# Four plain column tiles and five block pairs in the out-projection of a hybrid decoder layer

## The chip, the cores and the metric

The kernel runs on one core of a Trainium2 chip. The metric is the device time of one execution in microseconds (us): the median of three runs before the change is 2372.61 us (2370.54 to 2372.68).

## The reference, cut to what matters

A decoder layer over 16 learned tokens and 512 inputs, with 2048 features. Two head groups work side by side, a short convolution and a recurrent one; their 2048 output columns are multiplied by `w_out`, normalised and added to the input. A gated feed-forward layer follows. The change lies in the product with `w_out`.

```python
z = n @ w_in
y_conv = short_conv_group(z[..., :CONV_COLS], conv_w)
y_rwkv = rwkv7_group(z[..., CONV_COLS:], ...)
mix = jnp.concatenate([y_conv, y_rwkv], axis=-1) @ w_out      # 528 x 2048 by 2048 x 2048
h = h + rmsnorm(mix, g_post_mix)
f = conv_glu(rmsnorm(h, g_pre_ffn), w_gate_up, conv_ffn, w_down)
h = h + rmsnorm(f, g_post_ffn)
```

## The kernel before, in words

Everything is held transposed: 128 features on the partitions, tokens along the free axis. For the out-projection 514 tokens count, in two halves of 258 and 256 columns (`HY`). Products are made to float32 accuracy from two rounded parts of each operand, a high and a low one, as three matmuls: high by high, high by low, low by high.

The out-projection has 16 column tiles of 128 features each, `m` = 0 to 15, in three groups (lines 1384 to 1491):

- **Plain tiles**, `m` = 0 to `MS`-1 with `MS` = 6 (line 1386). `gemm` (line 552) goes over 16 feature tiles `k`, three part products and two token halves: 96 matmuls of 128x258 or 128x256. A tile's weights come as four chunks of 128x512 (`w_out`, 256 KB each); `wload` (line 543) loads a chunk into `raw` (three buffers, shared with other users), ScalarE casts the high part `whi` and VectorE subtracts to get the low part `wlo` (three buffers each).
- **Pairs**, four of them: `m` = 6 to 13, two tiles at a time (`pair`, line 1426). The weights of two tiles and the tokens are seen as 2 by 2 blocks, and the four products of blocks that two tiles need are made of seven products instead of eight. One product (`product`, line 1415) is 8 feature tiles by three part products, 24 matmuls of 258 columns, so a pair has 168. Its four weight blocks of 128x1024 (`w_pair`, 512 KB each) are loaded in the order a22, a21, a11, a12 into the tag `R`, which has five buffers; VectorE makes the sums and differences of blocks (`plus`, `less`), and `parted` (line 1352) makes a block's high part `H` and low part `O` (three buffers each). The first product of a pair uses a11 with tokens that are in place; the second a12; the third uses the token sums `T2`, the fifth `T3`, the sixth `T4`, and the last the block sum `s1` with `Y1`.
- **The last two tiles**, `m` = 14 and 15, by token halves.

The token sums that the pairs need are made once, by `sums(j)` for `j` = 0 to 7 (line 1371): two loads of 257 KB from `ysp` (the head groups' output in DRAM) into `R` (into `H` and `O` for `j` = 0), three VectorE sums or differences of 258 columns into `q`, `O` or `R`, and three splits, each a ScalarE cast and a VectorE subtraction into a `tt` block. Which plain tile a sum is made with stands in `JS` (line 85): `JS[m]` sums are written ahead of tile `m`. `Y1` is made after the plain tiles in a loop of eight (`again`, lines 1401 to 1408): a load into a `raw` buffer, a difference and a split that overwrites the tokens' second half, so it has to wait for the last plain tile to have read that half.

What sets the order: from line 1387 on, for `m` >= `MP` = 2, instructions are not issued as written but kept in a plan (`Plan`), and ordered by a list scheduler with modelled costs (`order`, `run`); the plan's start sets TensorE busy for the first `HEAD` = 8.0 us. The plan reaches from tile 2 over all pairs, the residual and the first feed-forward work, to line 1858. What is written before it, tiles 0 and 1 with what stands ahead of them, is placed by the framework's own scheduler, among the end of the plan before (the recurrent heads). The `matmul` steps carry the rank `FILL`: TensorE takes them when nothing of a higher rank is ready, so a plain tile's matmuls can lie between the products of a pair.

`layout` (lines 1992 to 1995) cuts `w_out` on the host by `MS`: columns of the plain and the last tiles as `w_out`, the rest as `w_pair`.

All engine calls go through one helper, so the profile shows every instruction at line 231; instructions are told apart by their tiles.

Of the kernel before, what the change touches and what calls it, by code (L numbers as in the profile page):

```python
# [78 lines left out]

K0, K1 = 4, 2  # L80

MS = 6


MP, JS, HEAD = 2, (0, 0, 3, 3, 2, 0), 8.0

GSUMS = (0, 4, 8, 12)

# [422 lines left out]
def hymba(tc, I, out, ysp=None):  # L511
# [40 lines left out]
    def gemm(src, mov, spans, first=None, into=None, kept=None, parts=1):  # L552


        for ku in range(KT // 4):
            if kept is not None:
                hi, lo = kept[ku]
            else:
                hi, lo = wload(src[ku], into and into[ku]) if ku or first is None else first
            for k4 in range(4):  # L560
                k = ku * 4 + k4
                ws = slice(k4 * 128, k4 * 128 + 128)
                xh, xl = mov[k]
                for pi, (w, x) in enumerate(((hi, xh), (hi, xl), (lo, xh))):
                    for o, a, b in spans:
                        PE.matmul(o, w[:, ws], x[:, a:b], start=(k == 0 and pi == 0),
                                  stop=(k == KT - 1 and pi == 2))
                    if pi == 2 or parts == 3:
                        yield

    def run(g):
        for _ in g:
            pass

    def fill(g):

        g = iter(g)
        while True:
            with plan.step(2, FILL):
                try:  # L580
                    next(g)
                except StopIteration:
                    return
            yield
# [669 lines left out]
    with ExitStack() as ctx2:  # L1254
# [43 lines left out]
        def mixed(x, m, i):  # L1298
            a, b = HY[i]
            sq[i] = ss[i] if m == 0 else small(b - a)  # L1300
            with plan.step(0 if m >= KT - 2 else 2):
                S.activation(out=sq[i], in_=x, func=AF.Square)
            if 0 < m < KT - 1:
                G.tensor_tensor(out=ss[i], in0=ss[i], in1=sq[i], op=ALU.add)
            S.activation(out=h[:, m, a:b], in_=x, func=AF.Copy, scale=pc("g_post", m))
# [26 lines left out]
        def half(ps, i):  # L1332
            a, b = HY[i]
            return [(ps[i][:, :b - a], a, b)]
# [50 lines left out]
        plan.head = HEAD  # L1385
        for m in range(MS):
            plan.on = m >= MP
# [38 lines left out]
        def pair(n):  # L1426


            a22, a21, a11, a12 = (load(I["w_pair"][n, i]) for i in (3, 2, 0, 1))
            s1 = big("R", F32)  # L1430
            plus(s1, a21, a22)
            k = two()

            def row(r, i, o, k=None):
                m = MS + 2 * n + r
                a, b = HY[i]
                o = o[:, 2 * i:]
                if k is not None:
                    plus(h[:, m, a:b], o, k[:, 2 * i:])
                    o = h[:, m, a:b]  # L1440
                mixed(o, m, i)

            c = product(a11, Y11, mp.tile([128, 2, 512], F32, name="mps")[:, 0, :258])
            S.copy(k[:, 0], c)
            row(0, 0, product(a12, Y21), k[:, 0])
            less(a11, s1, a11)
            product(a11, Y2, c, False)
            S.copy(k[:, 1], c)
            less(a21, a22, a11)
            less(a11, a12, a11)  # L1450
            plus(k[:, 1], product(a11, Y22), k[:, 1])
            product(a21, Y3, c, False)
            S.copy(k[:, 0], c)
            product(a22, Y4, c, False)
            row(1, 0, c)
            o = product(s1, Y1)
            row(0, 1, o, k[:, 1])
            row(1, 1, o, k[:, 0])

        for n in range((KT - 2 - MS) // 2):  # L1460
            pair(n)
# [4 lines left out]
        for n, m in enumerate(range(KT - 2, KT)):  # L1466
# [4 lines left out]
            else:  # L1471
                t = mp.tile([128, 2, 512], F32, name="mps")
                ps = [t[:, i] for i in range(2)]
            run(fill(gemm(I["w_out"][m - KT + 2 + MS], ys, half(ps, 0), into=keep)))
            mixed(half(ps, 0)[0][0], m, 0)
# [493 lines left out]
def layout(np, inp):  # L1969
# [6 lines left out]
    def tiles(w):  # L1976
        k, n = w.shape
        return w.reshape(k // 512, 4, 128, n // 128, 128).transpose(3, 0, 2, 1, 4).reshape(n // 128, k // 512, 128, 512)
# [13 lines left out]
    w = A["w_out"].reshape(KT, 128, D)[list(KORD)].reshape(D, D)  # L1992
    a, b = 128 * MS, D - 256
    r["w_out"] = tiles(np.concatenate([w[:, :a], w[:, b:]], axis=1))
# [51 lines left out]
```

## Time and profile before

| | before |
|---|---|
| median of three runs | 2372.61 us |
| the profiled execution's own time | 2370.47 us |
| its span, first to last instruction | 2368.7 us |
| first plain load of `w_out` / first load of `w_pair` | at 773.27 / 833.05 us |
| tile 2's first matmul | at 808.65 us |
| first pair's first matmul | at 848.30 us |

The span and the time of the same execution differ by 1.8 us. A row of a timeline has the start, the duration, the engine, the operation with `out<-in`, the shape, the count of merged instructions and, in brackets, the idle time of the engine before it with what ended it. Matmuls overlap: their pitch is read from the starts. A row of the stretches has, after the length, the busy time and count of TensorE (PE), its weight loads (PEld), VectorE (DVE), ScalarE (ACT) and GpSimd (POOL), then the granted TensorE clock, the share of the DMA engines and GB/s. SP is the queue that issues most DMAs; an SP row with several loads spans from the first issue to the last.

### The profile page before, as it was taken

The page shows a single profiled execution, that of the slowest core. Times are in us where ns is not written, and L with a number is a line of the kernel's source. Part 1 is how long each engine was busy: PE and PEld are TensorE (multiplying, and loading weights), DVE is VectorE, ACT ScalarE, POOL GpSimd, SP SyncE. Part 2 cuts the span into 40 slices and gives each one's busy share as a digit, 9 for nine tenths or more (in the row PEclk, how much of TensorE's full clock was granted, in tenths as well). Part 3 has the DMA queues.
Part 4 walks back from the last instruction along what each step waited for, and adds up shares of the span by engine and source line. Part 5 has one row for each costly group of instructions (what it writes and reads, how often), then busy time and mean ns, then how long its engine had stood idle before and what let it go on. Part 6 is the DMA issues. An engine that isn't in the chain of part 4 may idle for free.

```text
span 2368.7 us, 46298 instructions
## 1 busy us (share of the span) xinstructions
PE 2345.2 (99%) x18450; PEld 2238.2 (94%) x18450; DVE 1744.6 (74%) x2366; ACT 1225.2 (52%) x2402; POOL 636.1 (27%) x755
## 2 busy tenths in 40 slices
PE   9999999999999999999999999999999999999997
PEld 8999999999999999998989899999999998989897
DVE  7687888878754677784868686777767686859585
ACT  7666766766654555574434343343434342525255
POOL 0232747465351011510202121211212120202025
PEclk9999999999999999999999999999999999999998
DMA  5444332333433755913333323242423242323344
GB/s 185 158 126 122 90 97 83 104 111 98 132 99 95 232 170 178 214 57 100 108 107 103 112 82 124 81 134 81 124 75 125 70 135 79 124 82 105 97 142 90
DMA packets 138759, 274.14 MB, mean 116 GB/s; under 512 B 31120, under 2 KB 54288, under 8 KB 138544
## 3 DMA queue, kind: packets, MB, share of 16 engines
q1 hardware_dynamic: 131760, 264.35, 36.2%
q0 software_dynamic: 6784, 6.83, 2.0%
q8 instruction: 145, 2.38, 0.4%
q14 instruction: 70, 0.57, 0.1%
HBM read 245.30 MB, written 25.84 MB: 114 GB/s over the span
## 4 chain that ended last, share of the span: by engine, by line
PE 96%; DVE 1%; DMA 1%; POOL 1%; ACT 1%; issue 0%; DVEq 0%; SPq 0%; ACTq 0%; POOLq 0%
PE mps L231 60%; PE u L231 18%; PE d L231 11%; PE st L231 4%; PE aux L231 3%; DMA acc<-xT_dram 1%; DVE acc L231 0%; POOL acc L231 0%; PE psn L231 0%; DVE q L231 0%; DMA l<-lo 0%; DMA raw<-w_in_dram 0%; ACT whi L231 0%; POOL XR L231 0%; ACT q L231 0%
## 5 line engine op out<-in xcount | busy, mean ns | idle before, releaser
L231 ACT CAST H<-R 128x1024 fp32r<-128x1024 f32 x401 | 420.4, 1049 | 474.9 <-PE u L231 180.7
L231 DVE TENSOR_TENSOR O<-R,H 128x1024 fp32r<-128x1024 f32 x401 | 521.7, 1301 | 124.2 <-ACT H L231 116.8
L231 PE MATMUL mps<-ahi,whi 128*128 128x264 f32 (+2 forms) x1792 | 360.0, 289 | 6.1 <-ACT ahi L231 5.5
L231 PE MATMUL mps<-alo,whi 128*128 128x264 f32 (+2 forms) x1792 | 360.2, 289 | 0.0
L231 PE MATMUL mps<-ahi,wlo 128*128 128x264 f32 (+2 forms) x1792 | 358.0, 288 | 1.2 <-DVE wlo L231 1.0
L231 PE MATMUL mps<-tt,H 128*128 128x258 f32 x2160 | 288.2, 283 | 1.0 <-ACT q L231 0.9
L231 PEld LDWEIGHTS mps<-ahi,whi 128*128 128x128 f32 x1792 | 273.8, 189 | 9.1 <-ACT ahi L231 5.8
L231 PEld LDWEIGHTS mps<-ahi,wlo 128*128 128x128 f32 x1792 | 274.0, 189 | 3.6 <-DVE wlo L231 1.6
L231 PEld LDWEIGHTS mps<-alo,whi 128*128 128x128 f32 x1792 | 274.0, 189 | 2.8 <-DVE alo L231 0.6
L231 DVE TENSOR_TENSOR wlo<-raw,whi 128x512 fp32r<-128x512 f32 x261 | 199.2, 768 | 104.8 <-ACT whi L231 88.0
L231 PEld LDWEIGHTS mps<-tt,H 128*128 128x128 f32 x2160 | 272.6, 189 | 2.4 <-ACT q L231 1.1
L231 POOL TENSOR_TENSOR raw<-raw,rb 128x516 f32<-128x516 f32 (+1 forms) x45 | 92.8, 2062 | 668.7 <-DVE raw L231 630.6
L231 PE MATMUL mps<-alo,H 128*128 128x258 f32 x1064 | 258.3, 284 | 0.4 <-DVE alo L231 0.4
L231 PE MATMUL mps<-ahi,H 128*128 128x258 f32 x1064 | 258.0, 282 | 0.0
L231 POOL TENSOR_TENSOR R<-R 128x1024 f32<-128x1024 f32 x40 | 131.5, 3287 | 419.1 <-DVE R L231 419.1
L231 ACT CAST whi<-raw 128x512 fp32r<-128x512 f32 x261 | 160.7, 619 | 137.5 <-PE mps L231 83.9
L231 DVE TENSOR_TENSOR R<-R 128x1024 f32<-128x1024 f32 x136 | 226.4, 1665 | 1.7 <-DMA R<-w_pair_dram 0.4
L231 PEld LDWEIGHTS mps<-alo,H 128*128 128x128 f32 x1064 | 198.4, 189 | 0.9 <-DVE alo L231 0.6
L231 PEld LDWEIGHTS mps<-ahi,H 128*128 128x128 f32 x1064 | 198.7, 190 | 0.0
L231 POOL TENSOR_SCALAR SUV<-VT 32x64 f32<-32x64 f32 x272 | 129.4, 476 | 161.4 <-PE st L231 137.5
L231 PE MATMUL mps<-ahi,O 128*128 128x258 f32 x1064 | 157.5, 283 | 0.0
L231 PE MATMUL mps<-tt,O 128*128 128x258 f32 x1080 | 153.4, 281 | 0.0
(339 smaller groups left out, 4593.5 us busy)
## 6 DMA issues: line engine op xcount, KB each, us to landing
R<-w_gu_dram SPq DMA_DIRECT2D x176, 512.0 KB, 3.5
raw<-w_in_dram SPq DMA_DIRECT2D x208, 256.0 KB, 2.7
R<-w_down_dram SPq DMA_DIRECT2D x88, 512.0 KB, 3.7
raw<-w_out_dram SPq DMA_DIRECT2D x32, 256.0 KB, 3.6
R<-w_pair_dram SPq DMA_DIRECT2D x16, 512.0 KB, 4.3
l<-lo SPq DMA_DIRECT2D x24, 264.0 KB, 2.1
R<-ysp SPq DMA_DIRECT2D x14, 257.0 KB, 4.3
lo<-l SPq DMA_DIRECT2D x12, 264.0 KB, 2.6
```

The source lines that it names most:

```text
L231: return getattr(self.real, op)(*real, **{k: x.get() if isinstance(x, View) else x for k, x in kw.items()})
```

## The change

Two lines of constants:

```diff
-MS = 6
+MS = 4
-MP, JS, HEAD = 2, (0, 0, 3, 3, 2, 0), 8.0
+MP, JS, HEAD = 2, (0, 2, 3, 3), 8.0
```

Tiles 4 and 5 are no longer plain: the pairs now cover `m` = 4 to 13, five of them (`range((KT - 2 - MS) // 2)`, line 1460). The eight sums are written ahead of tiles 1, 2 and 3 (two, three, three) instead of 2, 3 and 4 (three, three, two). Since `MP` stays 2, the first two sums now stand outside the plan. The host layout follows `MS`: 24 chunks of `w_out` and 20 blocks of `w_pair` instead of 32 and 16. All else is as it was, though the plan from tile 2 on is made anew.

## The prediction

> **What bounds the kernel now.** I read the page first, for the bound, then the stretches around the out-projection, then the waits of TensorE there, then the timelines of TensorE, VectorE and SP for the places where the change bites.
>
> ```profile
> span 2368.7 us, 46298 instructions
> PE 2345.2 (99%) x18450; PEld 2238.2 (94%) x18450; DVE 1744.6 (74%) x2366; ACT 1225.2 (52%) x2402; POOL 636.1 (27%) x755
> ...
> raw<-w_out_dram SPq DMA_DIRECT2D x32, 256.0 KB, 3.6
> R<-w_pair_dram SPq DMA_DIRECT2D x16, 512.0 KB, 4.3
> ...
> R<-ysp SPq DMA_DIRECT2D x14, 257.0 KB, 4.3
> ```
>
> TensorE is busy for 99% of the span, so matmuls that go are worth their pitch, and any new wait of TensorE is paid in full. The loads' last column is the median from issue to landing. The out-projection, by stage (tile 2; tile 3; tiles 4 and 5 as far as the first pair; the first pair with the rest of tile 5):
>
> ```profile
> 808.65:820.20 11.55, 10.52 (x88) 10.31 (x87) 10.76 (x26) 7.76 (x20) 1.70 (x2) 1.00 0.81 264
> 820.20:831.80 11.60, 11.60 (x99) 11.60 (x98) 6.71 (x15) 6.27 (x15) 1.53 (x2) 1.00 0.61 190
> 831.80:848.30 16.50, 16.50 (x140) 16.50 (x138) 13.85 (x26) 10.28 (x22) 3.29 (x4) 1.00 0.72 237
> 848.30:874.50 26.20, 26.20 (x220) 26.20 (x219) 21.56 (x30) 12.15 (x23) 2.77 (x3) 1.00 0.51 159
> ```
>
> TensorE is full but for one place in tile 2. VectorE is nearly full in tile 2, then has room. The waits of TensorE between 760 and 1000 us are only these:
>
> ```profile
> PE mps L231 <- DVE wlo L231: 1.0, 1, 1.0
> PE mps L231 <- ACT q L231: 0.9, 1, 0.9
> PE mps L231 <- DVE alo L231: 0.4, 1, 0.4
> ```
>
> In TensorE's timeline the first is in tile 2, the second in the second pair:
>
> ```profile
> 808.65 0.40 PE L231 MATMUL mps<-ahi,whi 128*128 128x258 f32 x2
> ...
> 817.57 0.40 PE L231 MATMUL mps<-alo,whi 128*128 128x258 f32 x2
> 819.00 0.51 PE L231 MATMUL mps<-ahi,wlo 128*128 128x258 f32 x2 [1.03 <-DVE wlo L231]
> ...
> 848.30 1.13 PE L231 MATMUL mps<-ahi,H 128*128 128x258 f32 x8
> 849.27 1.11 PE L231 MATMUL mps<-alo,H 128*128 128x258 f32 x8
> ...
> 853.13 1.12 PE L231 MATMUL mps<-tt,H 128*128 128x258 f32 x8
> ...
> 883.26 1.96 PE L231 MATMUL mps<-tt,H 128*128 128x258 f32 x14 [0.86 <-ACT q L231]
> ```
>
> From 848.30 to 853.13 start five groups of eight matmuls: 4.83 us by 40, a pitch of 0.121 us. At 817.57 two matmuls start that need 0.24; the next starts 1.43 later, so the first wait costs 1.2 us in pitch.
>
> **The change part by part.** (1) Matmuls. Two plain tiles of 96 go, 192; one pair of seven products by 24 comes, 168. 24 fewer by 0.121 us: 2.9 us less. All lay on the path, TensorE being full on both sides.
>
> (2) Work beside it. Eight `w_out` chunks of 256 KB go, four `w_pair` blocks of 512 KB come: the same bytes. VectorE's added pair has seven `O` and four block differences, at the 1.2 us of the rows below some 13 us in a pair's 168 by 0.121 = 20.3 us; that fits, so in a pair well under way it costs nothing. A pair can wait for its bank as the second does (0.86 us, one of four pairs); one pair in four paid it, so for the fifth I take a quarter, rounded up, 0.3 us; bounds 0 and 0.9.
>
> (3) What the two plain tiles covered. This decides. Tiles 2 to 5 are TensorE's work while the token sums are made and the first pair's blocks arrive; now only tiles 2 and 3 are left, 192 matmuls by 0.121, 23.2 us from 808.65: to 831.8. When can the first pair start? The rows of VectorE, of SP, of the `w_pair` loads together, and of ScalarE:
>
> ```profile
> 809.87 0.98 DVE L231 TENSOR_TENSOR q<-R 128x258 f32<-128x258 f32 x1
> ...
> 817.93 0.42 DVE L231 TENSOR_TENSOR q<-R 128x258 f32<-128x258 f32 x1
> 818.27 0.68 DVE L231 TENSOR_TENSOR wlo<-raw,whi 128x512 fp32r<-128x512 f32 x1
> ...
> 825.83 0.42 DVE L231 TENSOR_TENSOR q<-R 128x258 f32<-128x258 f32 x1
> ...
> 837.69 0.41 DVE L231 TENSOR_TENSOR q<-R 128x258 f32<-128x258 f32 x1
> ...
> 843.10 1.22 DVE L231 TENSOR_TENSOR O<-R,H 128x1024 fp32r<-128x1024 f32 x1
> ```
> ```profile
> 804.38 0.80 SPq L231 DMA_DIRECT2D R<-ysp  x2
> ...
> 821.46 7.50 SPq L231 DMA_DIRECT2D raw<-w_out_dram  x4
> 829.06 1.04 SPq L231 DMA_DIRECT2D R<-ysp  x2
> ...
> 833.05 1.80 SPq L231 DMA_DIRECT2D R<-w_pair_dram  x3
> ```
> ```profile
> DMA to landing us min/median/max: 3.4/4.3/6.7
> ```
> ```profile
> 841.27 1.05 ACT L231 CAST H<-R 128x1024 fp32r<-128x1024 f32 x1 [0.25 <-DMA R<-w_pair_dram]
> ```
>
> The first sum starts at 809.87, the fourth at 817.93: three sums in 8.1 us with the data there, 2.7 us each, a `wlo` among them. The fifth starts only at 825.83, the eighth at 837.69: this second half is held back by SP, which from 821.46 to 829 is kept with four `w_out` chunks (for tiles 4 and 5) whose buffers come free at TensorE's pace, and only then issues the next sum's loads. Those four chunks are gone after the change, so SP is free there.
>
> What then limits the sums is the `R` ring: five buffers, two per sum, a load of 4.3 us and the sum's 2.7 us, so 7.0 us for two and a half sums, 2.8 us each. Eight from 809.87 end at 832.3, the seventh at 829.5. The first pair's a11 takes a buffer that the seventh frees; its load of 4.3 to 6.7 us (now the third of three, issued about 834.5, it ends just ahead of the cast at 841.27) lands at 833.8 to 836.2, the cast takes 1.05: 834.9 to 837.2 against 831.8. TensorE waits 3.1 to 5.4 us; I take 4.2. The wait does not add to one in tiles 2 and 3: if a weight chunk is late there, the sums go on meanwhile, and the wait ahead of the pair is as much shorter. So the 1.2 us of before lies inside the 4.2 and is taken off.
>
> Bounds from both sides: 0, below which a wait cannot go, if a11 gets a buffer ahead of the last sums; and 10.5 us, if a11 is ready no sooner than now, 841.27 + 1.05 = 842.3 less 831.8.
>
> (4) The sums' place. The two that stand ahead of tile 1 are outside the plan, with 4 loads, 6 sums or differences, 6 casts and 6 subtractions. They need not start earlier: the first load of the sums is at 804.38, behind the last recurrent head's memory, and its data begin the first sum at 809.87. But the plan now believes that the ring is empty when its own first sums begin, and puts them ahead of the low parts of tile 2 and 3. Behind a sum that waits for data stand, on VectorE, the `wlo` of the next chunk, and TensorE for that: the same mechanism as the wait at 819.00, longer now by up to two sums, 5.4 us. As said, this is another place for the same 4.2 us. On SP four loads now pass the plan's first ones; two issue in 0.80 us in the row above, so the chunks behind them come up to 1.6 us later, and that too would be part of the 4.2.
>
> (5) The first pair itself. The stretch from 848.30 shows VectorE busy 21.56 of 26.20 us, with the `Y1` loop and three low parts of tile 5 in it. Without these three (0.7 each) 19.5 us stand in the 20.3 us of a pair that no longer has a plain tile's matmuls between its products. That is tight: bounds 0 and 2 us (three of the differences of 0.4 us and one `O` on the path), nearest is the 0.86 us that the second pair lost, with VectorE less full; about half of it, 0.5, is taken.
>
> (6) The new order of all that follows. The plan reaches as far as before; waits of its later part may come or go, the 0.4 us above among them: ±1 us, taken as 0.
>
> Sum: -2.9 + 4.2 - 1.2 + 0.3 + 0.5 = +0.9 us on the profiled execution's 2370.47 us (span 2368.7, 1.8 us around it). That execution is 2.1 us under the median of 2372.61, so the median becomes **2373.5 us**. About 0.2%, 4.75 us, is what a measurement of this kernel can tell from no change; the forecast is no change.
>
> **The rivals.** (a) The first pair is covered in full: wait 0. For it speaks that after 821 SP has nothing but the sums to issue; against it that five buffers carry the sums and the first blocks alike. -2.9 - 1.2 + 0.3 = -3.8: 2368.8 us, still within 0.2%; past it only with the waits of 0.9 and 0.4 us gone too.
>
> (b) Slower: the sums keep the pace that they have now, because VectorE and ScalarE stand in their planned order behind weight parts that wait for TensorE (the fifth sum comes 8 us after the fourth in the rows above, and two `wlo` lie between). a11 is ready at 842.3, the wait is 10.5: -2.9 + 10.5 - 1.2 + 0.3 + 0.5 = +7.2, 2379.8 us. It is slower by over 0.2% from a wait of 8.0 us on, a11 ready after 839.8. Against it: the chunks that held SP and VectorE at that time are not there any more.
>
> (c) The wait lies in one piece and the clock falls. These stretches show the granted clock with the short wait in tile 2, and behind the kernel's last matmuls:
>
> ```profile
> 816.00:820.00 4.00, 2.97 (x25) 2.76 (x24) 3.97 (x11) 1.98 (x6) 0.00 (x0) 1.00 0.68 207
> ...
> 2355.00:2360.00 5.00, 0.34 (x2) 0.05 (x1) 3.62 (x9) 0.91 (x3) 3.22 (x4) 0.65 1.15 170
> 2360.00:2365.00 5.00, 0.00 (x0) 0.00 (x0) 4.76 (x8) 0.00 (x0) 2.93 (x4) 0.50 1.10 267
> ```
>
> One microsecond of idleness leaves it at 1.00; within some 5 us of nearly nothing it goes to 0.50. If the 4.2 us come in one piece and the clock needs as long to come back, half of 4.2 us is lost on top, 2.1: +3.0, 2375.6 us. No stretch shows how long it takes to come back. The Trainium skill, "TensorE: Matmul & The Clock Gate", section "Why this matters for your kernels", asks for no idle gaps over about 3 us between matmuls, else half rate; the last two rows agree with it, and no row here has such a gap ahead of more matmuls. By its window of 3.4 us (Part 1 of that page) the loss would be an estimated 1.7 us, +2.6 in all.
>
> **How the numbers follow.** Forecast, a wait of 3 to 5.4 us in pieces: 0.45. (a) 0.25, of which 0.05 goes past 0.2%. (b) 0.20. (c) 0.10, of which 0.03 is past 0.2% with a longer wait. So faster 0.05, same 0.45 + 0.20 + 0.07 = 0.72, slower 0.23. The forecast's own range is -0.2 to +2.1: 2372.4 to 2374.7. The whole range goes from (a)'s 2368.8 to (b)'s 2379.8, with little outside.
>
> **What would show it.** Right: 24 fewer matmuls; the first `w_pair` load at about 827 rather than 833; tiles 2 and 3 ending, with waits for `wlo` or `H`, some 4 us behind 831.8; the five pairs without long waits. Wrong: a first product at 832 with no wait on either side (a), or at 840 and later with the eighth sum near 837 (b), or a granted clock below 1.00 between 830 and 850 (c); or a loss over 1 us within the pairs, which (5) holds to be covered.

## The result, and the profile after

| | before | after |
|---|---|---|
| median | 2371.87 us (2370.54 to 2372.68, six runs) | 2389.93 us (2389.55 to 2392.98, six runs) |
| ratio to before | | 1.0079, 95% interval 1.0068 to 1.0089 |
| profiled execution, its span | 2370.47, 2368.7 us | 2390.04, 2388.2 us |

The change makes the kernel slower by 18.1 us, where +0.9 was forecast and +7.2 was the worst rival. The page of after, its span and the row of the engines:

```profile
span 2388.2 us, 46256 instructions
PE 2360.5 (99%) x18426; PEld 2240.8 (94%) x18426; DVE 1754.9 (73%) x2373; ACT 1229.6 (51%) x2404; POOL 639.1 (27%) x755
```

TensorE has 24 matmuls fewer and is busy 15.3 us longer. So most of the loss is no wait: the matmuls themselves take longer. To see which, both traces were divided at matmuls that both have (us; the same points serve all runs below):

| stretch | before | after | difference |
|---|---|---|---|
| start to the last matmul of the heads | 760.0 | 761.6 | +1.6 |
| out-projection, to its norm (1566 matmuls; 1542 after) | 190.8 | 193.9 | +3.0 |
| residual and start of the feed-forward, to the first product of 512 columns (1039) | 128.2 | 128.9 | +0.7 |
| feed-forward, to the last matmul (8865) | 1276.0 | 1289.9 | +13.9 |
| behind the last matmul | 13.7 | 14.0 | +0.4 |

The first row is the same work in both kernels; over all runs here it lay between 760.0 and 762.7, so its 1.6 us isn't the change's. The feed-forward, which the diff doesn't touch, has most of the loss. Two stretches of 1200 us in it, of before and then of after (columns as in the stretches above: length, TensorE, weight loads, VectorE, ScalarE, GpSimd, granted clock, DMA share, GB/s):

```profile
1100.00:2300.00 1200.00, 1200.00 (x8362) 1127.27 (x8361) 875.06 (x881) 485.61 (x631) 210.44 (x78) 1.00 0.33 102
```
```profile
1100.00:2300.00 1200.00, 1200.00 (x8228) 1115.85 (x8227) 859.92 (x865) 476.40 (x617) 204.93 (x76) 1.00 0.33 100
```

Nothing waits, the clock is 1.00, the other engines have room, and yet 134 matmuls fewer pass. TensorE's timeline, before and after: the first product of 512 columns, the starts of two later ones that lie 24 matmuls apart each, and the last group of the kernel's matmuls:

```profile
1079.01 0.40 PE L231 MATMUL u<-whi,H 128*128 128x512 f32 x1
...
1084.51 0.39 PE L231 MATMUL d<-whi,H 128*128 128x512 f32 x1
...
1089.97 0.39 PE L231 MATMUL u<-whi,H 128*128 128x512 f32 x1
...
2354.01 1.33 PE L231 MATMUL psn<-q,ones 128*128 128x192 f32 x4 [0.22 <-ACT q L231]
```
```profile
1084.28 0.40 PE L231 MATMUL u<-whi,H 128*128 128x512 f32 x1
...
1089.88 0.39 PE L231 MATMUL d<-whi,H 128*128 128x512 f32 x1
...
1095.48 0.39 PE L231 MATMUL u<-whi,H 128*128 128x512 f32 x1
...
2373.16 1.33 PE L231 MATMUL psn<-q,ones 128*128 128x192 f32 x4 [0.21 <-ACT q L231]
```

From the second to the third row, 24 matmuls: 5.46 us before (227.5 ns each), 5.60 after (233.3 ns). Added up from start to start, the feed-forward's 1920 products of 512 columns take 436.7 us before and 448.0 after, 11.3 more; the other 6945, nearly all of 258 columns, take 2.6 us more, 0.4 ns each. In the products of 512 and 258 columns the moving operand, the one that streams, is a token tile, and the stationary one, the weights, is a 128x128 piece of `H` or `O`.

What differs is where the tiles lie, `H` and `O` among them. The two sums that now stand ahead of tile 1 are the first code to ask the second pool for tiles, and `sums(0)` loads into `H` and `O`. The framework lays tiles out in the order of their first use. From the programs' allocation lists (bytes per partition):

```
         behind acc, in order                 H starts   mod 256   O starts   mod 256
before   q, R, H, O, tt1, tt0, tt2, hxl        150784       0       163072       0
after    H, O, q, tt0, tt1, tt2, R, hxl        124064     160       136352     160
```

A buffer of `H` or `O` has 4096 bytes and a stationary piece 512, so the remainder holds for every piece. The tiles around them move too: by the same lists `R`, from which `H` and `O` are made, goes from a multiple of 256 to 128 past one.

Now the out-projection, which the forecast was about. TensorE's waits between 760 and 1000 us in after:

```profile
PE mps L231 <- ACT whi L231: 2.7, 1, 2.7
PE mps L231 <- DVE wlo L231: 0.9, 1, 0.9
PE mps L231 <- issue: 0.5, 1, 0.5
PE mps L231 <- ACT tt L231: 0.4, 1, 0.4
PE u L231 <- ACT H L231: 0.3, 1, 0.3
```

TensorE's timeline shows the two longest in tile 2, whose first matmul is at 810.63, and the first pair's start:

```profile
816.60 0.51 PE L231 MATMUL mps<-ahi,whi 128*128 128x258 f32 x2 [2.65 <-ACT whi L231]
...
818.23 0.52 PE L231 MATMUL mps<-ahi,wlo 128*128 128x258 f32 x2 [0.89 <-DVE wlo L231]
...
819.80 0.63 PE L231 MATMUL mps<-alo,whi 128*128 128x258 f32 x2
820.23 0.63 PE L231 MATMUL mps<-ahi,wlo 128*128 128x258 f32 x2
...
840.31 1.22 PE L231 MATMUL mps<-ahi,H 128*128 128x258 f32 x8 [0.51 <-issue]
```

From 819.80 to 820.23 two matmuls take 0.43 us, 0.215 each instead of 0.121. The stretches of these microseconds say why:

```profile
812.00:816.00 4.00, 1.95 (x17) 1.74 (x15) 3.93 (x11) 2.90 (x10) 1.24 (x1) 1.00 0.80 273
816.00:819.20 3.20, 1.72 (x12) 1.51 (x12) 3.17 (x7) 1.78 (x5) 0.95 (x2) 1.00 0.80 240
819.20:822.60 3.40, 3.40 (x19) 3.40 (x18) 3.26 (x10) 2.19 (x6) 0.00 (x0) 0.50 0.92 289
822.60:826.00 3.40, 3.40 (x29) 3.40 (x29) 2.67 (x7) 1.53 (x4) 0.00 (x0) 0.99 0.84 250
```

The granted clock is 0.50 for 3.4 us behind the waits; some 16 matmuls lose 0.093 us each there, 1.5 us. Why `whi` is late shows first on SP. The `whi` that TensorE waits for is that of tile 2's second chunk. Its load before, and SP's rows after:

```profile
801.45 1.71 SPq L231 DMA_DIRECT2D raw<-w_out_dram  x2
```
```profile
797.03 4.12 SPq L231 DMA_DIRECT2D raw<-w_out_dram  x2
803.05 0.33 SPq L231 DMA_DIRECT2D ysp<-k  x1
806.19 0.33 SPq L231 DMA_DIRECT2D H<-ysp  x1
...
807.04 1.85 SPq L231 DMA_DIRECT2D R<-ysp  x4
808.93 1.14 SPq L231 DMA_DIRECT2D raw<-w_out_dram  x2
...
828.18 0.33 SPq L231 DMA_DIRECT2D R<-w_pair_dram  x1
```

Before, the load of that chunk was issued at 801.45, ahead of the sums' loads at 804.38. After, it stands behind the six loads of the sums at tile 1, and the first of these waits 2.6 us for the last head's store (`ysp<-k`) to land. So SP comes to the chunk at 808.93, 7.5 us later than before; 1.6 of that is the later end of the heads. No buffer held it: the `raw` buffer that it takes, that of the third chunk ahead of it, was free once the `wlo` in the first row below was done, at 803.6. VectorE and ScalarE after:

```profile
802.94 0.68 DVE L231 TENSOR_TENSOR wlo<-raw,whi 128x512 fp32r<-128x512 f32 x1
...
809.73 0.43 DVE L231 TENSOR_TENSOR q<-O,H 128x258 f32<-128x258 f32 x1 [4.72 <-DMA O<-ysp]
...
810.54 0.69 DVE L231 TENSOR_TENSOR wlo<-raw,whi 128x512 fp32r<-128x512 f32 x1
```
```profile
813.93 0.41 ACT L231 CAST tt<-R 128x258 fp32r<-128x258 f32 x1 [0.60 <-DVE R L231]
...
815.62 0.41 ACT L231 CAST tt<-q 128x258 fp32r<-128x258 f32 x1
815.93 0.61 ACT L231 CAST whi<-raw 128x512 fp32r<-128x512 f32 x1
...
839.16 1.05 ACT L231 CAST H<-R 128x1024 fp32r<-128x1024 f32 x1 [2.32 <-DMA R<-w_pair_dram]
```

The chunk lands at 813.9 by the trace, and ScalarE casts it only at 815.93, without a wait of its own: ahead of it stand a sum's cast that had waited for VectorE, four operations on tile 1's output and another sum's cast. Cast at once, `whi` would have been ready at 814.5, some 0.7 us after TensorE wanted it (an estimate from these rows). On VectorE the first sum stands 4.72 us at the head of the queue, waiting for its data, with a `wlo` behind it; that cost TensorE 0.2 us, at 811.28. The second of the two longest waits, 0.89 us, is for a `wlo` that VectorE makes at 817.50, behind steps of a sum. The last row is the cast of the first pair's a11.

### The profile page after: what moved, and what is told of

Read it like the earlier page. It is cut to its first block, busy times and chain, and to the rows that moved or that the text cites. A ratio compares the mean times of both kernels' runs of the same rounds, so it can differ in the third digit from the quotient of the medians.

```text
span 2388.2 us, 46256 instructions
## 1 busy us (share of the span) xinstructions
PE 2360.5 (99%) x18426; PEld 2240.8 (94%) x18426; DVE 1754.9 (73%) x2373; ACT 1229.6 (51%) x2404; POOL 639.1 (27%) x755
## 4 chain that ended last, share of the span: by engine, by line
PE 92%; DMA 3%; DVE 3%; issue 1%; ACT 1%; POOL 1%; SPq 0%; DVEq 0%; ACTq 0%; POOLq 0%
PE mps L231 56%; PE u L231 18%; PE d L231 11%; PE st L231 4%; PE aux L231 2%; DMA acc<-xT_dram 1%; DMA l<-lo 1%; DVE R L231 0%; DVE acc L231 0%; DMA R<-ysp 0%; DVE O L231 0%; POOL acc L231 0%; SPq L231 0%; DVE tt L231 0%; DVE q L231 0%
## 5 line engine op out<-in xcount | busy, mean ns | idle before, releaser
L231 ACT CAST H<-R 128x1024 fp32r<-128x1024 f32 x408 | 426.9, 1047 | 496.1 <-PE u L231 191.4
L231 DVE TENSOR_TENSOR O<-R,H 128x1024 fp32r<-128x1024 f32 x408 | 532.0, 1305 | 127.4 <-ACT H L231 115.7
L231 PE MATMUL mps<-ahi,whi 128*128 128x258 f32 (+1 forms) x1728 | 347.4, 289 | 8.8 <-ACT ahi L231 5.6
L231 PE MATMUL mps<-alo,whi 128*128 128x258 f32 (+1 forms) x1728 | 347.9, 289 | 0.1
L231 PE MATMUL mps<-ahi,wlo 128*128 128x258 f32 (+1 forms) x1728 | 346.0, 289 | 1.1 <-DVE wlo L231 0.9
L231 PE MATMUL mps<-tt,H 128*128 128x258 f32 x2208 | 295.2, 283 | 0.6 <-ACT tt L231 0.4
L231 PEld LDWEIGHTS mps<-tt,H 128*128 128x128 f32 x2208 | 279.1, 189 | 2.2 <-DVE tt L231 0.6
L231 PEld LDWEIGHTS mps<-ahi,whi 128*128 128x128 f32 x1728 | 264.5, 190 | 11.8 <-ACT ahi L231 5.6
L231 PEld LDWEIGHTS mps<-ahi,wlo 128*128 128x128 f32 x1728 | 264.4, 190 | 4.2 <-DVE wlo L231 2.1
L231 PEld LDWEIGHTS mps<-alo,whi 128*128 128x128 f32 x1728 | 264.5, 190 | 3.0 <-DVE alo L231 0.6
```

Source lines behind the costliest of these rows:

```text
L231: return getattr(self.real, op)(*real, **{k: x.get() if isinstance(x, View) else x for k, x in kw.items()})
```

## The experiments

The theory after the first comparison: two separate losses, the place of the weight tiles in memory (13.9 us in the feed-forward) and a shorter cover in the out-projection (some 3 us). The rival to the first: the new order of buffers, PSUM banks or phases of the rings behind the plan. "Stretches" below are out-projection, start of the feed-forward, feed-forward, as in the table above; before has 190.8, 128.2, 1276.0.

**The tiles' places exchanged.** `after_placed_as_before`: GpSimd writes eight columns of each buffer once, ahead of the sums, in the order of before's first uses; every tile then has before's address.

```diff
+            if m == 0:
+                for _ in range(3):
+                    G.memset(two()[:, 0, :8], 0.0)
+                for _ in range(5):
+                    G.memset(big("R", F32)[:, :8], 0.0)
+                for _ in range(3):
+                    G.memset(big("H", F32)[:, :8], 0.0)
...
```

> The changed kernel, with small memsets by GpSimd during tile 0 that touch q, R, H, O, tt1, tt0, tt2 in this order, so that every tile of the second pool lies at exactly the address that it had before the change; the order of buffers in their rings may differ. Theory P2 (the addresses are the cause): from the first 512-column matmul to the last matmul 1276 to 1277 us as before the change (1289.9 in the changed kernel), so 2373 to 2376 us in all: what the out-projection lost is left. Theory Q (the fifth pair, order of banks and rings): 1290 us, 2390 us.

Median 2377.45 us (2376.02 to 2382.76, seven runs), ratio 1.0028 (1.0017 to 1.0039). Stretches 193.6, 130.0, 1276.0: the feed-forward is back to the tenth, the out-projection stays at its loss. The median is a little above P2's 2373 to 2376 us.

```profile
1084.66 0.40 PE L231 MATMUL u<-whi,H 128*128 128x512 f32 x1
...
1090.16 0.39 PE L231 MATMUL d<-whi,H 128*128 128x512 f32 x1
```

24 matmuls in 5.50 us, as before's first 24 (1079.01 to 1084.51). The other way round, `before_placed_as_after` writes the same tiles in the order of after, in the kernel before (the same lines, with `H` and `O` first and `R` last).

> The kernel before with the same kind of memsets in the order H, O, q, tt0, tt1, tt2, R: the addresses of the changed kernel, and nothing else of the change. P2: 1290 us from the first 512-column matmul to the end, 2385 to 2387 us. Q: 1276 us, 2371 to 2373 us.

Median 2386.15 us (2385.82 to 2387.13), ratio 1.0061 (1.0046 to 1.0076). Stretches 191.8, 127.6, 1289.9.

```profile
1080.80 0.40 PE L231 MATMUL u<-whi,H 128*128 128x512 f32 x1
...
1086.40 0.39 PE L231 MATMUL d<-whi,H 128*128 128x512 f32 x1
```

5.60 us, as after's first 24 (1084.28 to 1089.88). So the place alone, with before's sums, order and tiles, costs the feed-forward 13.9 us. The rival falls: the order of the work in `before_placed_as_after` is not that of after, and the feed-forward takes the same 1289.9.

**Which places are good.** Five kernels move `H` and `O` by some bytes. `after_ho_plus64` puts 64 bytes ahead of `H`, `after_ho_plus32`, `after_ho_plus96` and `after_ho_plus224` put 32, 96 or 224 bytes ahead of `H` and 32 more behind `q`; `before_plus32` puts 32 bytes ahead of all these tiles in the kernel before. The diff is that of `after_ho_plus32`; eight floats are 32 bytes.

```diff
+            if j == 0:
+                V.memset(p2.tile([128, 8], F32, name="pad2", bufs=1), 0.0)
...
+            if m == 0:
+                V.memset(p2.tile([128, 8], F32, name="pad", bufs=1), 0.0)
```

> Control: the changed kernel with one unused tile of 64 bytes ahead of H, which moves H, O and all behind them by 64 bytes, with the remainders by 64 unchanged. P, Q and R: 2390 us, 512-column matmuls at 233 ns. If this is as quick as the one with 32 bytes, the remainder by 64 is not what matters.

> The changed kernel with two unused tiles of 32 bytes per partition (two tiny memsets) that move the weight tiles H and O, and q, by 32 bytes in SBUF, to addresses that divide by 64, as H and O had before the change; all other tiles keep their remainder by 64. Theory P (H and O at 32 past a multiple of 64 make the matmuls of the feed-forward layer slower): the 512-column matmuls go back from 233.3 to about 227.5 ns, about 15 us are gained, 2373 to 2376 us. Theory Q (the fifth pair or the new order shifts the rotation of buffers and banks): 2390 us. Theory R (it matters in which region H and O lie, not the remainder): 2390 us.

> The changed kernel with H and O moved by 96 bytes, to the remainder by 512 that they had before the change (256), all else by 128 bytes; still in the changed kernel's region. If the remainder by 512 (or 128) is what matters: 512-column matmuls at 227 ns and 2373 to 2376 us. If the region or the distance to the other operand matters too: 230 to 233 ns, 2380 to 2390 us.

> The kernel before with 32 bytes of padding ahead of the tiles q, R, H, O and tt: H starts at 150816 instead of 150784 bytes (remainder by 256: 32 instead of 0); instructions, order and waits as before. Theory (the start address of the weight tiles sets the pitch of the feed-forward's matmuls): the stretch from the first 512-column matmul to the last goes from 1276 us to about 1290, the median from 2371.3 to about 2385. Rival (the order of the buffers in memory, or which tile lies beside which, sets it): no change, 2371 to 2373, since the order is that of before.

> The changed kernel with 224 bytes of padding ahead of H and 32 behind q, so that H starts at 124288 (remainder by 512: 384) and the tiles q, O, tt, R lie in the order of after. Theory 1 (a remainder that is a multiple of 128 is enough): the feed-forward's stretch takes 1276 us, the median is 2374 to 2376. Theory 2 (a multiple of 256 is needed): about 1282 as with the remainder 192, or more; median 2380 to 2384. Rival (the distance from the place of after counts, not the remainder): near 1290, 2390.

| kernel | `H`, `O` mod 256 | feed-forward | median (its range) | ratio to before |
|---|---|---|---|---|
| before | 0 | 1276.0 | 2371.87 | |
| after_placed_as_before | 0 | 1276.0 | 2377.45 | 1.0028 (1.0017 to 1.0039) |
| after_ho_plus96 | 0 | 1275.8 | 2374.84 (2373.72 to 2378.22) | 1.0015 (1.0006 to 1.0025) |
| before_plus32 | 32 | 1287.2 | 2383.56 (2382.57 to 2384.58) | 1.0053 (1.0036 to 1.0069) |
| after_ho_plus224 | 128 | 1286.5 | 2387.21 (2386.31 to 2387.53) | 1.0066 (1.0051 to 1.0081) |
| after | 160 | 1289.9 | 2389.93 | 1.0079 (1.0068 to 1.0089) |
| before_placed_as_after | 160 | 1289.9 | 2386.15 | 1.0061 (1.0046 to 1.0076) |
| after_ho_plus32 | 192 | 1282.4 | 2382.89 (2382.43 to 2384.58) | 1.0048 (1.0033 to 1.0063) |
| after_ho_plus64 | 224 | 1290.2 | 2391.73 (2389.88 to 2392.76) | 1.0084 (1.0069 to 1.0099) |

Both places at a multiple of 256 give 1276, though they lie 26 KB apart and the tiles around them are in another order; each of the five other remainders tried costs 6 to 14 us. The multiple of 64 (192) wins back about half of the loss, the multiple of 128 less: both of those guesses fall. `before_plus32` keeps before's order and shows the loss, so it isn't the order.

Two of these kernels part `H` and `O` from most tiles around them. By their allocation lists `after_ho_plus32` and `after_ho_plus64` have `R`, `hxl` and the `tt` tiles at the same addresses, and only `q`, `H` and `O` lie 32 bytes apart; their feed-forwards take 1282.4 and 1290.2 us. So these 7.8 us are not `R`'s. The good place is less well fenced in: in both kernels `H` and `O` start 256 past a multiple of 512, and `R` at a multiple of 256 as well. No other multiple of 256 was tried.

The first 24 products of 512 columns in `before_plus32`, then in `after_ho_plus96`:

```profile
1079.95 0.39 PE L231 MATMUL u<-whi,H 128*128 128x512 f32 x1
...
1085.52 0.40 PE L231 MATMUL d<-whi,H 128*128 128x512 f32 x1
```
```profile
1085.06 0.40 PE L231 MATMUL u<-whi,H 128*128 128x512 f32 x1
...
1090.55 0.39 PE L231 MATMUL d<-whi,H 128*128 128x512 f32 x1
```

5.57 and 5.49 us. `after_ho_plus96` is the changed kernel with nothing mended but the place, and it lies 0.15% above before.

**The moving operand.** `before_tokens_minus32` shifts the token parts `ahi` and `alo` of the kernel before by 32 bytes, to multiples of 64, with `H` and `O` where they were.

```diff
-    ones = cp.tile([128, 1], F32, name="ones")
-    z0 = cp.tile([128, 1], F32, name="z0")
+    oz = cp.tile([128, 2], F32, name="oz")
+    ones, z0 = oz[:, :1], oz[:, 1:]
...
+    V.memset(wp.tile([128, 8], F32, name="pad", bufs=1), 0.0)
```

> The kernel before with the token tiles ahi and alo, which the matmuls of 258 columns stream, moved by 32 bytes, from 32 past a multiple of 64 to a multiple of 64; the weight tiles H and O stay. If the streamed operand's remainder by 64 matters as well: 258-column matmuls by 1 to 2 ns quicker than 119.5, 2355 to 2365 us, faster than both kernels. If only the weights' place matters: 2371 to 2373 us.

Median 2375.01 us (2372.15 to 2376.91), ratio 1.0012 (1.0003 to 1.0022); stretches 191.9, 128.0, 1278.4. Neither forecast holds: no gain, rather 2.4 us more in the feed-forward, 2.1 of them in the products of 258 columns. A multiple of 64 doesn't help these tokens.

That the place of a moving tile can count as much, for its own products, shows in `hxl`, which streams in 160 products of 512 columns. Before, it starts 128 past a multiple of 256, and these products have a mean pitch of 234.2 ns; the 160 that stream `hxh`, which starts at a multiple, against the same `H` have 226.7. In `after_ho_plus96` `hxl` starts at a multiple too, and its products have 226.7. They are few: 7.5 ns each make 1.2 us.

**The sums' place.** `before_sums_at_tile1` keeps six plain tiles and four pairs and moves only the sums, as the change does.

```diff
-MP, JS, HEAD = 2, (0, 0, 3, 3, 2, 0), 8.0
+MP, JS, HEAD = 2, (0, 2, 3, 3, 0, 0), 8.0
```

> The kernel before with only the sums' places changed: JS = (0, 2, 3, 3, 0, 0), six plain tiles and four pairs as before. The sums at tile 1 make H and O the first tiles behind acc, at the same addresses as in the changed kernel. P and R: the feed-forward layer is slower by the same 14 to 15 us, 2385 to 2388 us. Q by the fifth pair: 2371 to 2374 us.

Median 2392.61 us (2391.58 to 2393.55), ratio 1.0089 (1.0073 to 1.0106); stretches 197.2, 128.4, 1289.9. The line of constants alone brings both losses: the tiles lie as in after, and TensorE stands 5.3 us, until 824.7, for a `whi`; the forecast had not counted that wait, and the median lies above its 2385 to 2388 us. The clock behind the wait:

```profile
825.00:828.00 3.00, 3.00 (x15) 3.00 (x16) 2.93 (x8) 1.65 (x4) 0.00 (x0) 0.50 0.85 247
```

`four_plain_sums_at_2_3` has four plain tiles and no sum ahead of tile 1: all eight stand in the plan. `H`, `O` and `R` lie as before.

```diff
-MP, JS, HEAD = 2, (0, 2, 3, 3), 8.0
+MP, JS, HEAD = 2, (0, 0, 4, 4), 8.0
```

> The changed kernel with JS = (0, 0, 4, 4): four plain tiles and five pairs, but all sums inside the plan, where the first loads go to R; H and O get the addresses that they had before the change. P and R: the feed-forward layer runs as before the change, and what is left is the out-projection: 2.9 us of matmuls less, waits of 3 to 8 us more, 2371 to 2378 us. Q by the fifth pair: 2388 us or more.

Median 2380.26 us (2379.41 to 2381.80), ratio 1.0036 (1.0023 to 1.0049); stretches 197.0 (with 15 matmuls that in after come behind the dividing point, some 1.8 us), 127.6, 1277.2. The feed-forward is back to before's time but for 1.2 us; the median is 2 us above the forecast. Tile 2 has no wait; they now lie at the first pair, 3.2 us ahead of it and 2.1 and 1.0 us inside the pairs.

`after_four_ahead` and `after_one_ahead` have before's places, and four or one of the sums ahead of tile 1: `(0, 4, 2, 2)` and `(0, 1, 4, 3)` in the same line.

> The changed kernel with its tiles placed as before and the eight sums spread 0, 4, 2, 2 over the four plain tiles instead of 0, 2, 3, 3. Theory (the three sums in tile 2 stand in VectorE's order ahead of a low part of the weights, and TensorE waits for that one, which also brings the half clock): with one sum fewer in tiles 2 and 3 each, the wait of 2.8 us there falls under 1.5 us, the clock stays at 1.00, and the out-projection's stretch takes 191 to 192 us instead of 193.6; median 2374 to 2376 instead of 2377.5. Rival (the ring of R buffers and the loads of the sums set the pace, wherever the sums stand): the wait moves, into tile 1 or ahead of the first pair, with the same sum of 4 us or more; 193 to 196 us, median 2377 to 2380.

Median 2380.51 us (2379.58 to 2382.77), ratio 1.0040 (1.0025 to 1.0055); stretches 201.0, 128.4, 1276.0. The theory's 191 to 192 us fails, and so does the size that the rival gave. TensorE's waits there:

```profile
PE mps L231 <- ACT whi L231: 7.0, 1, 7.0
PE mps L231 <- DVE wlo L231: 2.7, 1, 2.7
```

Both lie inside tile 2 (at 815.70 and 828.24): fewer sums in the plan don't help, for with more sums ahead of it the wait for the weight parts is longer.

> The changed kernel with its tiles placed as before and the sums spread 0, 1, 4, 3 over the four plain tiles instead of 0, 2, 3, 3. With four sums ahead of tile 1 the first wait, at the first product of tile 2, was 7.3 us, with two 2.9 us, with none the wait lay ahead of and inside the first pair. Theory (the place of the wait follows the spread, and only its pieces matter for the clock): with one sum there it is 0.3 to 1.5 us, one to two more lie ahead of the first pair, no piece is over 2 us, the clock stays at 1.00, and the out-projection's stretch is 191 to 192.5 us; median 2374 to 2376, within 0.2% of before. Rival (the sum of the waits grows with whatever order): 5 us of waits or more, a half clock, 193.5 us or more, median 2377 or more.

Median 2377.42 us (2376.48 to 2378.69), ratio 1.0027 (1.0016 to 1.0038); stretches 195.5, 128.1, 1276.0. The waits in tile 2 are short now, as the theory had it, but the one ahead of the first pair is 5.2 us and not one to two; the rival's numbers hold. Its longest waits, and the stretches about the last of them:

```profile
PE mps L231 <- POOL hxh L231: 5.2, 1, 5.2
PE mps L231 <- DVE wlo L231: 1.2, 2, 1.0
```
```profile
836.00:840.00 4.00, 0.02 (x1) 0.00 (x0) 3.52 (x8) 1.70 (x5) 1.64 (x2) 1.00 0.99 370
840.00:844.00 4.00, 2.81 (x13) 2.85 (x14) 3.15 (x4) 2.46 (x3) 0.80 (x1) 0.66 0.53 203
```

TensorE stands still while VectorE is nearly full and the DMA engines' share is 0.99. GpSimd's `hxh`, which the row names, can't be all of it: a11's cast, without which the pair has no weights, runs at 840.04, 1.02 us after ScalarE's last work, when its load lands.

So the waits of the out-projection sum to 5.6 us in after, and 5.5 in `after_placed_as_before` (two, three, three), 7.7 with all sums in the plan, 11.3 with four ahead, 8.0 with one, against 2.2 before (each a matmul's pitch less 0.12 us, where that is over 0.14). None of the spreads hides them. No kernel tried beats before; the best of the changed ones is `after_ho_plus96`, 1.0015.

## Why the prediction was wrong

- **(1) Matmuls, right.** 24 fewer, 2.9 us less.
- **(3) and (4), the cover: cause right, path and size only in part.** From tile 2's first matmul at 810.63, 23.2 us without a wait end at 833.8; the first pair starts at 840.31, 6.5 us late, where 4.2 was forecast. 4.7 of the 6.5 are waits (2.8, 1.0, 0.2 and 0.7), 1.5 the half clock. The sums' new place is the cause, as (4) said. But the path that (4) priced highest, a `wlo` on VectorE behind a sum that waits for data, "up to two sums, 5.4 us", cost 0.2 and 0.9 us. The longest wait came by the path that it put at "up to 1.6 us": SP's chunk behind the sums' loads came 5.9 us later, the heads' later end left out, since those loads waited for the last head's store, and 2.0 us on ScalarE, which the prediction didn't have, were added. The first load of `w_pair` came at 828.18 (about 827 forecast, 833.05 before). Against the forecast, most of the wait lay in tile 2 and little ahead of the pair.
- **(c), the clock, fell, though its condition was not met.** It fell to 0.50 at 819, not between 830 and 850, and lost 1.5 us beside (c)'s 2.1. The prediction gave this 0.10 as a rival to waits "in pieces"; the waits did come in pieces, 2.65 and 0.89 us, and the clock fell all the same. The Trainium skill, "TensorE: Matmul & The Clock Gate", Part 1, has a window of 3.4 us for going either way, and the length of the row at 0.50, 3.4 us, agrees. Its rule in "Why this matters for your kernels", no idle gap over about 3 us, wasn't enough here: neither wait was as long. In `after_placed_as_before`, where one wait took 3.8 us, the clock stayed at 0.50 for twice that length, 6.9 us (816.7 to 823.6).
- **(2) and (5), the pairs: sizes right.** 0.4 and 0.3 us of waits at the pairs' `u` products, where (5) had 0.5 and (2) 0.3. Before's 0.9 in the second pair is gone, which was not forecast.
- In sum the out-projection took 3.0 us more (2.8 with the tiles placed as before) where +0.9 was forecast: 3.4 of waits and 1.5 of clock less 2.9 of matmuls make 2.0. Of the other 1.0, 0.7 is in nine matmuls of about 0.22 us, most of them the first behind a wait (two before), and 0.3 in 0.2 ns more on each of the rest.
- **(6), the step that failed.** "The new order of all that follows. The plan reaches as far as before; waits of its later part may come or go, [...] ±1 us, taken as 0." It looked for waits alone. The stretch behind the out-projection, where waits could come or go, did take +0.7. But the prediction held the matmuls' duration behind the plan to be given, and it depends on where their operands lie; the tiles' addresses follow the order of first use, which `JS` changed. It cost 13.9 us, shown by `after_placed_as_before` and `before_placed_as_after`.

With the place mended, the change costs 0.15% in `after_ho_plus96` (3.5 us above the 2371.33 of the runs of before beside it) and 0.28% in `after_placed_as_before` (6.1 us), where +0.9 us was forecast. The first, 2374.84 us, is 0.1 us above the forecast's own range. That it comes so near is in part luck: its out-projection takes 193.8 us, 3.0 more than before, as in after.

Open: why TensorE is slower with other places. The experiments moved `H` and `O` with all that writes and reads them, so that it is the read of the weights, and not, say, its meeting with ScalarE's writes to the same buffers, is not shown. Nor is the slowness even: in after the products of 258 columns that stream `alo` against `H` have 120.1 ns, 1.2 less than before, while those that stream `wlo` against `H`, of 512 columns, have 236.2, 9.2 more. With `hxl` above, this speaks for something between the two operands' places, but no run settles it. Nor is the order of the remainders explained (192 better than 128). Over all runs the start of the feed-forward varies from 127.6 to 130.5 us; what sets that was not tried.

## What to carry to other kernels

When TensorE is full and its matmuls change pitch in a stage that the edit doesn't touch, compare the addresses of its operands, the stationary tiles first, before looking for waits: here an edit that only moved a first use shifted them, and the two good places were worth 6 to 14 us in 1290 against the five others. Pin the layout (ask for the tiles in a fixed order, or pad) before judging any edit to the schedule; unpinned, this change looked three to five times as bad as its own mechanism makes it (0.79% against 0.28 and 0.15%). And work that waits for data, placed earlier in a queue, delays all that stands behind it: here the loads of two sums held up a weight chunk by some 6 us, and moving sums earlier only moved TensorE's wait.

## What the runs showed of the hardware that was not expected

- The pitch of a 128x512 fp32r matmul depends on where its operands start: 227.5 ns in before's second 24, with `H` and `O` at a multiple of 256 bytes, 233.3 ns in after's, with both at 160 past one; and with `H` as before, 226.7 ns where the moving tile is at a multiple of 256 and 234.2 where it is 128 past one.
- The length of a single wait does not tell whether the clock falls. In `four_plain_sums_at_2_3` a single wait of 3.2 us, in the first row below, left it at 1.00 behind it:

```profile
834.00:838.00 4.00, 0.97 (x8) 0.80 (x8) 3.88 (x10) 3.35 (x9) 0.98 (x1) 1.00 0.98 364
838.00:841.00 3.00, 2.88 (x24) 2.67 (x22) 2.96 (x3) 0.31 (x3) 1.03 (x1) 1.00 0.64 252
841.00:844.40 3.40, 1.54 (x9) 1.54 (x10) 3.33 (x4) 2.99 (x4) 0.00 (x0) 0.85 0.00 0
844.40:847.80 3.40, 3.40 (x21) 3.40 (x21) 3.40 (x6) 1.75 (x4) 0.00 (x0) 0.65 0.00 0
```

It fell only behind the next one of 2.1 us; in after, 2.65 and 0.89 us within 5 us were enough. Whether waits add up, or it matters at which moment they come, no run here separates.
